# Input projection of a two-layer trunk: low-rank rows transposed before their norm, and three wide column sections in place of five

## The chip, the cores and the metric

The kernel runs on one core of one Trainium2 chip. The metric is the device time of one execution in microseconds (us), lower is better. Three runs of the kernel before gave 2254.48 to 2260.23 us, median 2259.06 us.

## The reference, cut to what matters

Two layers work on 512 latent and 256 context tokens of width 1024. Each layer projects the normed tokens to 2400 columns, cuts them into pieces, mixes the tokens in four ways (multi-head latent attention, neighbourhood attention, a bidirectional S5 recurrence, retention), and follows with a mixture of experts. The change touches the projection and the attention's two low-rank pieces, 192 columns of queries (cq) and 128 of keys and values (ckv):

```python
pl = split_cols(hl @ w_in[layer])
...
def mla_queries(cq, g_cq, w_uq, cos, sin):
    q = (rmsnorm(cq, g_cq) @ w_uq).reshape(B, L, MLA_HEADS, MLA_NOPE + MLA_ROPE)
...
def mla_keys_values(ckv, kr, g_ckv, w_ukv, cos, sin):
    kv = (rmsnorm(ckv, g_ckv) @ w_ukv).reshape(B, L, MLA_HEADS, MLA_NOPE + MLA_V)
...
def softmax_attention(q, k, v):
    s = jnp.einsum('bqhd,bkhd->bhqk', q, k, preferred_element_type=F32)
    p = jax.nn.softmax(s, axis=-1).astype(v.dtype)
```

`rmsnorm` multiplies each token's row by one number, the inverse root of its mean square. That number can also be applied after the matrix product.

## The kernel before, in words

One layer is `mixer`, then `moe`. In `mixer` the normed tokens lie transposed in SBUF, split into a high and a low part (`hTh`, `hTl`). A product with `w_in` is three matmuls (`mm3`, L202 to L204): high by high, high by low, low by high. The weights arrive raw by DMA on SP's queue (`wload`, L493) in pieces of half a section, into three buffers (`w_raw`). `wnext` splits each piece: ACT casts the high part (`w_hi`, L196), POOL subtracts it from the raw weights (`w_lo`, L197). `w_hi` and `w_lo` have four buffers each, two sections.

The projection goes in this order. First 256 columns for S5, transposed (`s5_in`); its result goes through DRAM into the tile `U`. Then the 1376 columns that are wanted with tokens on the partitions (`proj_nat`), in five sections of 288 or 272 columns (`SECS`); within a section each of the six token tiles takes 24 matmuls (8 chunks of the contraction by 3). In layer 1 the two context tiles skip columns that nobody needs. Last come three sections of 256 transposed columns (`proj_last`: keys, gate and queries).

S5 is woven in between. `s5_states` makes the states: matmuls `s_v` (L778) with matrices `Fg` that are read from DRAM by SP's queue (L775, two buffers), three copies of ACT into `H` for each, and then one long chain of small DVE operations on `H`: L790 to L793 seven steps within blocks of eight, L798 to L801 eleven steps over blocks, L806 to L809 the correction. ACT shifts the result into `HP` (L815 to L817). `s5_out` multiplies `HP` (matmuls `s_y`, L836 to L838, with `TPg` and `Eg` from SP's queue), applies the gelu, sends the result through DRAM into `GT`, and multiplies again (`s_z`, L858). `S5AT` says after which section each of the two is recorded; a list scheduler then sets every engine's order. In the kernel before they are recorded after section 0 and after section 2.

The two low-rank pieces go through `mla_prep` in every token tile: ACT squares the PSUM result and sums it (L1037), DVE adds epsilon (`rs_a`, L224), POOL raises it to the power of minus a half (`rs_b`, L226), DVE multiplies (`acn`, L1039), PE transposes it (`a_t`, L1042 and L1044), ACT applies the gains (`cqT`, `ckT`). The transposes are recorded a tile later (`flush`). In `mla_qkv` and `mla_attn`, some 140 us later, these feed the keys, values and queries and the softmax (`softmax`, L1002 to L1007).

Of the kernel before, what the change touches and what calls it, by code (L numbers as in the profile page):

```python
# [9 lines left out]
F32 = mybir.dt.float32  # L10
F32R = mybir.dt.float32r
# [4 lines left out]
ALU = mybir.AluOpType  # L16
# [18 lines left out]
SECS = (0, 288, 560, 832, 1104, 1376)  # L35
# [95 lines left out]
N_RQ, N_KR, N_CQ, N_NV, N_CKV, N_NW, N_RK, N_RV = 0, 256, 288, 480, 560, 688, 864, 1120  # L131
# [3 lines left out]
_ORDER = ("rq", "kr", "cq", "nv", "ckv", "nw", "rk", "rv", "u", "nq", "nk", "rg")  # L135
# [29 lines left out]
class Trunk:  # L165

    NB = ((7, 4, 3), (7, 6, 0))
    S5AT = ((0, 2), (0, 2))
# [156 lines left out]
    def mixer(self, l):  # L325
        tc, nc = self.tc, self.nc
        nt = self.nt
        with ExitStack() as left, ExitStack() as right:
            mS = self.pool("mS", es=left)
            self.mxS = mS.tile([P, 2, 2, nt * P], F32R, name="mixS")  # L330
            with ExitStack() as proj:
# [44 lines left out]
                with ExitStack() as sx:  # L376
                    na = self.pool("na", 2, es=sx, side="right")
                    self.s5u = self.pool("s5u", es=sx, side="right")
                    w = self.wnext()
                    self.s5_in(w, natP, self.s5u)  # L380
                    self.mla_prep_load(na)
                    for s in range(5):
                        self.proj_nat(s, na, tabs)
                        if s == self.S5AT[l][0]:
                            for _ in tabs:
                                pass
                            tb.close()
                            s5p, s5w = self.pool("s5p", es=sx, side="right"), self.pool("s5w", 2, es=sx, side="right")
                            self.s5_states(s5p, s5w)
                        if s == self.S5AT[l][1]:  # L390
                            self.s5_out(s5p, s5w)
# [124 lines left out]
    def proj_nat(self, s, na, side):  # L516
# [481 lines left out]
    def softmax(self, n, src, wk, tag):  # L998
# [6 lines left out]
        nc.scalar.activation(out=p, in_=src, func=AF.Exp, bias=nm, accum_out=s)  # L1005
# [61 lines left out]
    def mla_qkv(self, ap, aw):  # L1067
# [11 lines left out]
        self.aV = ap.tile([P, NT, 4, 64], F32, name="aV")  # L1079
        for i in range(NT):  # L1080
# [4 lines left out]
            nc.vector.tensor_copy(kf[:, :, 0:64], pv[:, :, 0:64])  # L1085
            nc.scalar.copy(out=self.aV[:, i], in_=pv[:, :, 64:128])
# [14 lines left out]
    def mla_attn(self, i, ap, aw):  # L1101
# [5 lines left out]
        for hp in range(2):  # L1107
            pTs = []
            for h in (2 * hp, 2 * hp + 1):
# [4 lines left out]
                p = self.softmax(T - k0, ps[:, :T - k0], aw, "a")  # L1114
# [765 lines left out]
def _layout(i):  # L1880
# [48 lines left out]
```

## Time and profile before

| what | value |
|---|---|
| median of three runs | 2259.06 us |
| the profiled execution's own time | 2260.11 us |
| its span, first to last instruction | 2258.3 us |
| busy: PE, DVE, ACT, POOL | 1955.8, 933.0, 499.6, 370.0 us |
| mean granted TensorE clock | 0.938 of full speed |
| projection and S5, layer 0 | about 92 to 299 us |
| projection and S5, layer 1 | about 1295 to 1488 us |
| attention of layer 0 | around 440 to 520 us |

The share of busy time is an average over stages with different limits; most of the span belongs to the experts, which the change does not touch. A row of a timeline gives the start, the duration, and in brackets how long the engine sat idle before and what ended that. A row of the windows gives each engine's busy time within a stretch (PE, its weight loads, DVE, ACT, POOL) and the clock that TensorE was granted in it: 1.00 is 2.4 GHz, 0.50 is 1.2 GHz. "issue" is an idle time for which the profile shows no releaser.

### The profile page before, as it was taken

The numbers are of one execution on the slowest core, as the hardware profiler recorded it, in microseconds if no ns is written. First come the engines' busy times: TensorE is split into PE (matmuls) and PEld (weight loads), VectorE is DVE, ScalarE is ACT, GpSimd is POOL, SyncE is SP. The second block draws the span as 40 slices with busy tenths as digits, with TensorE's granted clock in tenths as the row PEclk, the third lists the DMA queues.
The fourth block names the chain that finished last, engine by engine and source line by source line (L and its number), as shares of the span: only waits on it lengthen the run. The fifth ranks groups of instructions, "written<-read, shape, count | busy, mean of one in ns | idle before, by whom it ended". The sixth has DMA issues, their size and how long they took to land. (4 is left out here: it accounts for less than half of the span.)

```text
span 2258.3 us, 32874 instructions
## 1 busy us (share of the span) xinstructions
PE 1955.8 (87%) x12609; PEld 1161.1 (51%) x12609; DVE 933.0 (41%) x2175; ACT 499.6 (22%) x1095; POOL 370.0 (16%) x396
## 2 busy tenths in 40 slices
PE   5897988899869879989887887988896898998996
PEld 2787865457733323333332687855475454444443
DVE  3758156463425411111111529056544353453444
ACT  3342232251202200000001521332432111111111
POOL 2532252120100000000001322253302000000000
PEclk9898999999979999999998988989997899999998
DMA  7351355562568999999998441355617599999996
GB/s 271 107 150 44 83 175 195 194 202 71 191 248 305 376 391 375 385 375 362 373 373 342 154 105 49 83 166 192 202 59 269 216 395 419 419 420 418 419 420 255
DMA packets 160477, 578.55 MB, mean 256 GB/s; under 512 B 30032, under 2 KB 71504, under 8 KB 111152
## 3 DMA queue, kind: packets, MB, share of 16 engines
q1 hardware_dynamic: 123344, 530.69, 61.8%
q10 hardware_dynamic: 31296, 31.36, 4.5%
q0 software_dynamic: 5664, 14.23, 2.2%
q8 instruction: 104, 1.70, 0.3%
q14 instruction: 69, 0.57, 0.1%
HBM read 536.33 MB, written 43.42 MB: 257 GB/s over the span
## 5 line engine op out<-in xcount | busy, mean ns | idle before, releaser
L1671 PE MATMUL e_pa<-ew,hT 128*64 128x512 f32 x1664 | 424.4, 605 | 39.0 <-DMA ew<-in_moe_w 32.5
L1671 PEld LDWEIGHTS e_pa<-ew,hT 128*64 128x64 f32 x1664 | 126.2, 139 | 299.0 <-issue 245.1
L1695 PE MATMUL e_py<-ew,aT 128*64 128x512 f32 x832 | 207.1, 632 | 10.6 <-DVE aT L1687 7.8
L226 POOL TENSOR_TENSOR rs_b<-rs_a,mhalf 128x1 f32<-128x1 f32 (+1 forms) x58 | 38.2, 658 | 834.5 <-DVE rs_a L224 829.5
L202 PE MATMUL nat_ps<-w_hi,hTh 128*128 128x272 f32 (+3 forms) x480 | 149.4, 311 | 9.0 <-ACT nat L190 5.5
L1676 ACT ACTIVATE sA<-e_pa 64x512 f32<-64x512 f32 x52 | 30.8, 592 | 564.0 <-PE e_pa L1671 549.9
L1677 DVE TENSOR_TENSOR sA<-sA,e_pa 64x512 f32<-64x512 f32 x52 | 35.9, 690 | 277.2 <-ACT sA L1676 276.7
L204 PE MATMUL nat_ps<-w_hi,hTl 128*128 128x272 f32 (+3 forms) x480 | 147.1, 306 | 0.0
L203 PE MATMUL nat_ps<-w_lo,hTh 128*128 128x272 f32 (+3 forms) x480 | 146.8, 306 | 0.0
L197 POOL TENSOR_TENSOR w_lo<-w_raw,w_hi 128x1024 fp32r<-128x1024 f32 (+2 forms) x36 | 89.9, 2509 | 234.2 <-ACT w_hi L196 109.7
L1695 PEld LDWEIGHTS e_py<-ew,aT 128*64 128x64 f32 x832 | 59.0, 143 | 113.9 <-issue 95.2
L1557 POOL DMA_INDIRECT hg<-hd,stok x32 | 31.3, 980 | 446.2 <-PE hg_t L1569 411.9
L202 PEld LDWEIGHTS nat_ps<-w_hi,hTh 128*128 128x128 f32 x480 | 98.9, 206 | 10.7 <-ACT nat L190 6.4
L296 PE MATMUL mod_ps<-wmod,cT 128*32 128x256 f32 x768 | 80.1, 444 | 27.2 <-DMA wmod<-in_w_mod 27.2
L192 DVE COPY hT<-hg_t 128x256 f32<-128x256 f32 (+2 forms) x45 | 24.0, 534 | 192.0 <-PE e_pa L1671 160.6
L203 PEld LDWEIGHTS nat_ps<-w_lo,hTh 128*128 128x128 f32 x480 | 98.7, 206 | 0.4 <-issue 0.4
L204 PEld LDWEIGHTS nat_ps<-w_hi,hTl 128*128 128x128 f32 x480 | 98.4, 205 | 0.2 <-issue 0.2
L203 PE MATMUL tr_ps<-hTl,w_hi 128*128 128x256 f32 (+1 forms) x256 | 88.1, 344 | 11.0 <-POOL hTl L486 10.6
L202 PE MATMUL tr_ps<-hTh,w_hi 128*128 128x256 f32 (+1 forms) x256 | 88.1, 344 | 5.4 <-DVE gT L583 3.3
L204 PE MATMUL tr_ps<-hTh,w_lo 128*128 128x256 f32 (+1 forms) x256 | 85.5, 334 | 0.0
L1017 PE MATMUL pT_ps<-const,sm_p 128*128 128x128 f32 x352 | 57.6, 292 | 18.4 <-DVE sm_p L1007 12.1
L1642 DVE TENSOR_TENSOR xr<-xr,po_ps 128x512 f32<-128x512 f32 x104 | 67.1, 684 | 7.7 <-PE po_ps L1640 7.1
(471 smaller groups left out, 3530.6 us busy)
## 6 DMA issues: line engine op xcount, KB each, us to landing
ew<-in_moe_w SPq DMA_DIRECT2D x384, 1024.0 KB
wmod<-in_w_mod SPq DMA_DIRECT2D x96, 512.0 KB
yd<-zero SPq DMA_DIRECT2D x20, 512.0 KB
w_raw<-in_w_in SPq DMA_DIRECT2D x16, 544.0 KB
w_raw<-in_w_in SPq DMA_DIRECT2D x16, 512.0 KB
w_raw<-in_w_out SPq DMA_DIRECT2D x32, 256.0 KB
yd<-yA ACTq DMA_DIRECT2D x64, 128.0 KB
hd<-h ACTq DMA_DIRECT2D x10, 512.0 KB
```

The costliest lines, as they stand in the source:

```text
L197: (eng or self.nc.vector).tensor_tensor(out=lo, in0=src, in1=_f(hi), op=ALU.subtract)
L202: mm(out, lhsT=lh, rhs=rh, start=start, stop=False)
L203: mm(out, lhsT=lh, rhs=rl, start=False, stop=False)
L204: mm(out, lhsT=ll, rhs=rh, start=False, stop=stop)
L226: nc.gpsimd.tensor_tensor(out=r, in0=t, in1=self.mhalf[:, :n], op=ALU.pow)
L296: nc.tensor.matmul(ps[32 * j:32 * j + 32, 256 * q:256 * q + 256], lhsT=self.cT[:, k], rhs=w[:, j], start=(k == 0), stop=(k == KD - 1))
L1017: nc.tensor.transpose(pt[:, b], p[:, (a + b) * P:(a + b + 1) * P], self.ident)
L1557: self.nc.gpsimd.indirect_dma_start(out=hg, out_offset=None, in_=self.hd[0:n], in_offset=bass.IndirectOffsetOnAxis(ap=idx, axis=0), bounds ...
L1642: nc.vector.tensor_tensor(out=x, in0=x, in1=ps, op=ALU.add)
L1671: mm(pa[64 * j:64 * j + 64], lhsT=hT[k][:, 0:64], rhs=(w1, w3)[j][k], start=(k == 0), stop=(k == KD - 1))
L1677: nc.vector.tensor_tensor(out=sA, in0=sA, in1=pa[64:128], op=ALU.mult)
L1695: mm(py[64 * j:64 * j + 64, 0:512], lhsT=aT[:, k * 64:(k + 1) * 64], rhs=w2[k][:, h * 512:(h + 1) * 512], start=(k == 0), stop=(k == 3))
```

## The change

It does four things. (1) `mla_prep` copies the low-rank rows out of PSUM unnormed and transposes these; the sums of squares go into one tile of 12 columns for the layer (`cms`), and one `rsqrt` on it in `mla_qkv` gives all factors. The key and value factor is multiplied in where `kf` and `aV` leave PSUM; the query factor joins in the softmax, as a scale of the exponential and one more multiplication of the negated maximum for each of the 40 heads and tiles. (2) `proj_nat` has three sections of 464, 464 and 448 columns. The column order changes, so that a tile's results leave PSUM in eight pieces and not nine. (3) The weights come in quarters: each piece has half as many chunks, three raw buffers, five `w_hi` and six `w_lo` (four make a section). (4) The S5 parts are recorded after tile 3 of section 0 and after tile 4 of section 1.

```diff
-SECS = (0, 288, 560, 832, 1104, 1376)
+SECS = (0, 464, 928, 1376)
...
-    S5AT = ((0, 2), (0, 2))
+
+    S5AT = ((0, 3), (1, 4))
...
-        r = self.W.tile([P, 4, w], F32, tag="raw", name="w_raw", bufs=3)
...
+        r = self.W.tile([P, 2, w], F32, tag="raw", name="w_raw", bufs=3)
...
-        for a in range(2):
-            hi = self.W.tile([P, 4, w], F32R, tag="whi", name="w_hi", bufs=4)
-            lo = self.W.tile([P, 4, w], F32R, tag="wlo", name="w_lo", bufs=4)
+        for a in range(4):
+            hi = self.W.tile([P, 2, w], F32R, tag="whi", name="w_hi", bufs=5)
+            lo = self.W.tile([P, 2, w], F32R, tag="wlo", name="w_lo", bufs=6)
...
+            then(s, i)
...
+        if scale is not None:
+            nc.vector.tensor_tensor(out=nm, in0=nm, in1=scale, op=ALU.mult)
...
-        nc.scalar.activation(out=t[:, :w], in_=ps[:, :w], func=AF.Square, scale=w ** -0.5, accum_out=ss)
-        r = self.rsqrt(aw, ss, 1, 1.0, "ar")
-        nc.vector.tensor_scalar(out=t[:, :w], in0=ps[:, :w], scalar1=r, scalar2=None, op0=ALU.mult)
+        nc.scalar.copy(out=t[:, :w], in_=ps[:, :w])
         yield
+        sq = aw.tile([P, 192], BF16, tag="asq", name="asq", bufs=1)
+        nc.scalar.activation(out=sq[:, :w], in_=t[:, :w], func=AF.Square, scale=w ** -0.5, accum_out=self.cms[:, i + (0 if q else NT):i + (1 if q else NT + 1)])
...
+        rn = self.rsqrt(self.cp, self.cms, 2 * NT, 1.0, "ar")
+        self.rq, rk = rn[:, :NT], rn[:, NT:]
...
-            nc.vector.tensor_copy(kf[:, :, 0:64], pv[:, :, 0:64])
-            nc.scalar.copy(out=self.aV[:, i], in_=pv[:, :, 64:128])
+            nc.vector.tensor_scalar(out=kf[:, :, 0:64], in0=pv[:, :, 0:64], scalar1=rk[:, i:i + 1], scalar2=None, op0=ALU.mult)
+            nc.scalar.mul(out=self.aV[:, i], in_=pv[:, :, 64:128], mul=rk[:, i:i + 1])
...
-                p = self.softmax(T - k0, ps[:, :T - k0], aw, "a")
+                p = self.softmax(T - k0, ps[:, :T - k0], aw, "a", self.rq[:, i:i + 1])
```

Three places of the order that the scheduler sets. The first is SP's queue in layer 0 around the loads of `Fg` (each row a DMA; the numbers are those of buffers). Before:

```order
L493 DMA w_raw_764<-in_w_in 128x1088
L493 DMA w_raw_1518<-in_w_in 128x1088
L493 DMA w_raw_1524<-in_w_in 128x1088
L493 DMA w_raw_1771<-in_w_in 128x1088
L493 DMA w_raw_1777<-in_w_in 128x1088
L493 DMA w_raw_2179<-in_w_in 128x1088
L775 DMA Fg_1234<-s5f0_308 128x4x128
L775 DMA Fg_1244<-s5f0_308 128x4x128
L832 DMA TPg_2020<-s5k0_307 16x4x128 x3
L775 DMA Fg_1254<-s5f0_308 128x4x128
L775 DMA Fg_1264<-s5f0_308 128x4x128
```

With the change:

```order
L496 DMA w_raw_794<-in_w_in 128x928
L779 DMA Fg_1220<-s5f0_312 128x4x128
L779 DMA Fg_1230<-s5f0_312 128x4x128
L496 DMA w_raw_1566<-in_w_in 128x896
L496 DMA w_raw_1572<-in_w_in 128x896
L779 DMA Fg_1240<-s5f0_312 128x4x128
L779 DMA Fg_1250<-s5f0_312 128x4x128
L496 DMA w_raw_1578<-in_w_in 128x896
L496 DMA w_raw_1584<-in_w_in 128x896
L779 DMA Fg_1260<-s5f0_312 128x4x128
L779 DMA Fg_1270<-s5f0_312 128x4x128
L779 DMA Fg_1280<-s5f0_312 128x4x128
```

Before, all raw weights ahead stand in front of the `Fg` loads and none between them; with the change quarters of section 2 stand between the pairs of `Fg`.

The second is PE in layer 0 around the first matmuls on `HP` (L837 before, L841 with the change). Before:

```order
L203 MATMUL nat_ps_2480<-w_lo_2365,hTh_93 128x272
L837 MATMUL s5_y_2029<-HP_1503,Eg_2016 128x96
L204 MATMUL nat_ps_2480<-w_hi_2364,hTl_94 128x272
...
L204 MATMUL nat_ps_2480<-w_hi_2370,hTl_94 128x272
L202 MATMUL nat_ps_2506<-w_hi_2364,hTh_93 128x272
...
L838 MATMUL s5_y_2029<-HP_1503,Eg_2017 128x96
...
L204 MATMUL nat_ps_2506<-w_hi_2364,hTl_94 128x272
```

With the change:

```order
L205 MATMUL nat_ps_2170<-w_hi_2016,hTl_94 128x448
L841 MATMUL s5_y_1813<-HP_1489,Eg_1800 128x96
L203 MATMUL nat_ps_2170<-w_hi_2022,hTh_93 128x448
...
L205 MATMUL nat_ps_2170<-w_hi_2022,hTl_94 128x448
L203 MATMUL tr_ps_2230<-hTh_93,w_hi_2206 128x512
...
L842 MATMUL s5_y_1813<-HP_1489,Eg_1801 128x96
...
L203 MATMUL tr_ps_2230<-hTh_93,w_hi_2212 128x512
```

Before, 16 and 24 `nat_ps` matmuls of 272 columns come behind it (the rest of a tile and a whole tile); with the change 6 of 448 columns do, and then the section of the keys (`tr_ps`).

The third is PE in layer 0 between the last `s_y` (L838, now L842) and the first `s_z` (L858, now L862). Before:

```order
L838 MATMUL s5_y_2110<-HP_1503,Eg_2098 128x96
L203 MATMUL tr_ps_2606<-hTl_94,w_hi_2548 128x512
...
L202 MATMUL tr_ps_2632<-hTh_93,w_hi_2542 128x256
...
L202 MATMUL tr_ps_2670<-hTh_93,w_hi_2658 128x512
...
L202 MATMUL tr_ps_2698<-hTh_93,w_hi_2658 128x256
...
L202 MATMUL tr_ps_2726<-hTh_93,w_hi_2658 128x512
...
L204 MATMUL tr_ps_2726<-hTh_93,w_lo_2665 128x512
L858 MATMUL s5_z_2143<-GT_2134,wglu_2137 128x384 x2
```

With the change:

```order
L842 MATMUL s5_y_1894<-HP_1489,Eg_1882 128x96
L203 MATMUL tr_ps_2358<-hTh_93,w_hi_2334 128x512
...
L203 MATMUL tr_ps_2386<-hTh_93,w_hi_2334 128x256
...
L203 MATMUL tr_ps_2414<-hTh_93,w_hi_2334 128x512
...
L205 MATMUL tr_ps_2414<-hTh_93,w_lo_2353 128x512
L862 MATMUL s5_z_1927<-GT_1918,wglu_1921 128x384 x2
```

Before, the last group of `s_y` stands in the keys' third tile (`tr_ps_2606`), and 5 matmuls of 512 columns, 24 of 256, 24 of 512, 24 of 256 and 21 of 512 follow before `s_z`; with the change it stands three matmuls into the first tile of the gate (`tr_ps_2358`), and 21 of 512, 24 of 256 and 24 of 512 follow.

## Rows read from the trace of the kernel before

**Rows 1.** Windows by stage: window, length, engine busy us (instructions), TensorE clock, DMA share, GB/s

```profile
155.20:218.90 63.70, 52.10 (x371) 50.41 (x370) 59.49 (x173) 11.79 (x33) 12.91 (x9) 0.92 0.24 74
222.10:299.05 76.95, 72.82 (x437) 64.05 (x437) 8.60 (x12) 21.02 (x34) 17.50 (x15) 0.98 0.32 84
1295.26:1345.80 50.54, 43.75 (x294) 42.99 (x293) 5.87 (x30) 13.63 (x39) 15.00 (x17) 0.83 0.46 115
1345.80:1411.30 65.50, 52.10 (x367) 50.90 (x366) 60.48 (x175) 12.39 (x40) 14.17 (x11) 0.87 0.17 50
1414.60:1488.00 73.40, 71.76 (x435) 62.89 (x435) 8.26 (x11) 21.75 (x32) 19.69 (x13) 1.00 0.33 84
```

**Rows 2.** Waits of PE, 92 to 240 us: waiter, releaser, total us, times, longest

```profile
PE a_t L1042 <- DVE acn L1039: 6.1, 4, 2.5
PE s_y L837 <- issue: 1.8, 1, 1.8
```

**Rows 3.** The same, 1295 to 1440 us

```profile
PE a_t L1042 <- DVE acn L1039: 11.0, 3, 7.1
PE s_y L837 <- issue: 1.6, 1, 1.6
```

**Rows 4.** Timeline of PE: start us, us, operation; the first HP matmuls of layer 0

```profile
220.03 0.29 PE L203 MATMUL nat_ps<-w_lo,hTh 128*128 128x272 f32 x1
222.14 0.43 PE L837 MATMUL s_y<-HP,Eg 128*128 128x96 f32 x2 [1.82 <-issue]
```

**Rows 5.** Timeline of PE: 96 matmuls of 288 columns, 24 of 512

```profile
1295.26 0.30 PE L202 MATMUL nat_ps<-w_hi,hTh 128*128 128x288 f32 x1
...
1308.06 0.18 PE L202 MATMUL nat_ps<-w_hi,hTh 128*128 128x32 f32 x1
...
1450.39 0.40 PE L202 MATMUL tr_ps<-hTh,w_hi 128*128 128x512 f32 x1
...
1455.85 0.28 PE L202 MATMUL tr_ps<-hTh,w_hi 128*128 128x256 f32 x1
```

**Rows 6.** Groups of DVE by shape inside the chain of layer 0, 155.2 to 218.9 us

```profile
L1039 DVE TENSOR_SCALAR acn<-nat_ps,rs_b 128x128 f32<-128x128 f32 x5 | 1.7, 350 | 1.2 <-POOL rs_b L226 1.2
L224 DVE TENSOR_SCALAR rs_a<-ass 128x1 f32<-128x1 f32 x5 | 0.8, 153 | 0.0
```

**Rows 7.** Timeline of DVE: the same operation alone and beside a split

```profile
172.08 0.58 DVE L793 TENSOR_TENSOR H<-H,rt 128x192 f32<-128x192 f32 x1
...
174.77 2.58 DVE L793 TENSOR_TENSOR H<-H,rt 128x192 f32<-128x192 f32 x1
```

**Rows 8.** Timeline of POOL: the splits inside that chain

```profile
174.45 2.49 POOL L197 TENSOR_TENSOR w_lo<-w_raw,w_hi 128x1088 fp32r<-128x1088 f32 x1
203.61 4.69 POOL L197 TENSOR_TENSOR w_lo<-w_raw,w_hi 128x1024 fp32r<-128x1024 f32 x2 [20.26 <-ACT w_hi L196]
```

**Rows 9.** Timeline of PE: last L838 of layer 0, then its first L858

```profile
251.47 0.39 PE L838 MATMUL s_y<-HP,Eg 128*128 128x96 f32 x2
...
269.33 0.88 PE L858 MATMUL s_z<-GT,wglu 128*128 128x384 f32 x2 [0.29 <-DVE GT L846]
```

**Rows 10.** Timeline of PE in layer 1: the wait for Fg

```profile
1332.18 1.57 PE L778 MATMUL s_v<-U,Fg 128*128 128x96 f32 x6 [4.07 <-DMA Fg<-s5f]
```

**Rows 11.** Timeline of SP's queue ahead of that wait

```profile
1327.38 0.35 SPq L493 DMA_DIRECT2D w_raw<-in_w_in  x1
1327.83 1.16 SPq L775 DMA_DIRECT2D Fg<-s5f  x2
```

**Rows 12.** Windows: after that wait, and the attention stage

```profile
1332.20:1340.80 8.60, 8.60 (x48) 8.60 (x49) 0.00 (x0) 3.28 (x11) 0.00 (x0) 0.61 0.36 118
...
440.00:520.00 80.00, 77.25 (x446) 45.85 (x445) 47.30 (x98) 41.26 (x97) 21.20 (x19) 0.97 0.49 162
```

**Rows 13.** Waits of the SP queue, 40 to 310 us

```profile
SPq L493 <- POOL w_lo L197: 111.5, 12, 22.2
```

**Rows 14.** Groups of DVE by shape, 440 to 520 us

```profile
L1006 DVE RECIPROCAL sm_s<-sm_s 128x1 f32<-128x1 f32 x20 | 3.2, 159 | 4.9 <-ACT sm_p L1005 4.8
```

More of the change, by code (lines that the diff above doesn't have):

```diff
@@ L381, in mixer, with then @@
                     self.mla_prep_load(na)
-                    for s in range(5):
-                        self.proj_nat(s, na, tabs)
-                        if s == self.S5AT[l][0]:
+                    def then(s, i):
+                        if (s, i) == self.S5AT[0]:
                             for _ in tabs:
@@ L387, in mixer @@
                             tb.close()
[L388 to L391, printed above, removed]
+                            self.s5p, self.s5w = self.pool("s5p", es=sx, side="right"), self.pool("s5w", 2, es=sx, side="right")
+                            self.s5_states(self.s5p, self.s5w)
+                        if (s, i) == self.S5AT[1]:
+                            self.s5_out(self.s5p, self.s5w)
+                    for s in range(len(SECS) - 1):
+                        self.proj_nat(s, na, tabs, then)
                 nat2 = self.pool("nat2", es=rt, side="right")
@@ L489, in wload @@
     def wload(self, c0, w, a):
-        r = self.W.tile([P, 4, w], F32, tag="raw", name="w_raw", bufs=3)
-        o = c0 * D + a * 512 * w
-        self.nc.sync.dma_start(out=r.rearrange("p k n -> p (k n)"), in_=self.I["w_in"][self.l, o:o + 512 * w].rearrange("(p n) -> p n", p=P))
+        r = self.W.tile([P, 2, w], F32, tag="raw", name="w_raw", bufs=3)
+        o = c0 * D + a * 256 * w
+        self.nc.sync.dma_start(out=r.rearrange("p k n -> p (k n)"), in_=self.I["w_in"][self.l, o:o + 256 * w].rearrange("(p n) -> p n", p=P))
         return r
@@ L497, in wstart @@
         self.secs = [(T_U, 256)] + [(a, b - a) for a, b in zip(SECS[:-1], SECS[1:])] + [(T_NK, 256), (T_RG, 256), (T_NQ, 256)]
-        self.ahead = [self.wload(*self.secs[0], a) for a in range(2)]
+        self.ahead = [self.wload(*self.secs[0], a) for a in range(4)]
     def wnext(self):
@@ L509, in wnext @@
                 ahead.append(self.wload(*self.secs[0], a))
-            for k in range(4):
+            for k in range(2):
                 his.append(hi[:, k])
@@ L514, in wnext, with proj_nat @@
         return his, los
-    def proj_nat(self, s, na, side):
+    def proj_nat(self, s, na, side, then):
         nc = self.nc
@@ L530, in proj_nat @@
             self.flush()
-            next(side, None)
-            next(side, None)
+            for _ in range(3):
+                next(side, None)
             for p0, w, dst in ((N_RQ, 256, self.nat[:, i, 0]), (N_KR, 32, None), (N_CQ, 192, None), (N_NV, 80, 0), (N_CKV, 128, None),
@@ L995, in retention, with softmax @@
             yield
-    def softmax(self, n, src, wk, tag):
+    def softmax(self, n, src, wk, tag, scale=None):
         nc = self.nc
@@ L1024, in mla_prep_load @@
         self.krt = [self.load_const(na, n) for n in ("krc", "krs")]
+        self.cms = self.cp.tile([P, 2 * NT], F32, tag="cms", name="cms%d" % l)
+        nc.gpsimd.memset(self.cms, 1.0)
         self.gq = na.tile([P, 3], F32, name="gcq", bufs=1)
@@ L1032, in mla_prep @@
         nc, gq = self.nc, self.gq
-        w = 192 if which == N_CQ else 128
+        q = which == N_CQ
+        w = 192 if q else 128
         tk = slice(i * P, (i + 1) * P)
-        ss = aw.tile([P, 1], F32, tag="ass", name="ass")
         t = aw.tile([P, 192], F32, tag="acn", name="acn")
-        nc.scalar.activation(out=t[:, :w], in_=ps[:, :w], func=AF.Square, scale=w ** -0.5, accum_out=ss)
-        r = self.rsqrt(aw, ss, 1, 1.0, "ar")
-        nc.vector.tensor_scalar(out=t[:, :w], in0=ps[:, :w], scalar1=r, scalar2=None, op0=ALU.mult)
+        nc.scalar.copy(out=t[:, :w], in_=ps[:, :w])
         yield
+        sq = aw.tile([P, 192], BF16, tag="asq", name="asq", bufs=1)
+        nc.scalar.activation(out=sq[:, :w], in_=t[:, :w], func=AF.Square, scale=w ** -0.5, accum_out=self.cms[:, i + (0 if q else NT):i + (1 if q else NT + 1)])
         pt = self.pT.tile([P, 512], F32, tag="T", name="a_t")
```

10 lines of the change are left out of this document (5 added, 5 removed).

## The prediction

> **What bounds the kernel now.** I read the windows by stage first, then the waits of PE in the two projection stages, then the timelines of DVE, POOL and PE at the places where a wait ends. The experts, most of the span, are untouched, so the question is two stages of about 200 us each.
>
> I cut each at the chain's start and at `s_y`; the windows of layer 1 show all three parts, those of layer 0 the last two [rows 1]. In the middle part DVE is busy 59.49 of 63.70 us in layer 0 and 60.48 of 65.50 us in layer 1: that is S5's chain, from its first multiplication at 155.2 (1345.8) to its last addition at 218.9 (1411.3). PE is busy 52 us in it and loses time in small waits: 6.1 us for `acn` in layer 0, 11.0 in layer 1 [rows 2, 3]. These look like the cost that the change takes away. But PE also waits at the end of the chain, 1.8 and 1.6 us at the first `s_y` on `HP` [rows 2, 3]; in layer 0 the matmul before it starts at 220.03, and it starts at 222.14, 3.2 us after the chain's end at 218.9 [rows 4]. (The profile calls that releaser "issue"; the ACT copies into `HP` lie in these 3.2 us.) So PE's small waits and the chain end together: **the chain sets the time, and PE's slack is already used up**. The reader should see that taking work or waits from PE ahead of `s_y` moves them into the wait at `s_y`. What counts is when the chain starts, how long it is, and what PE must still do behind it.
>
> **The change, part by part.** Matmuls: five sections become three, so the two layers' 1440 matmuls become 864 for the same columns. 96 matmuls of 288 columns take 12.80 us, 0.1333 each, and 24 of 512 take 5.46, 0.2275 each [rows 5]; between them 464 columns come to 0.208, 448 to 0.201, 272 to 0.127. Layer 0: 144 x 0.1333 + 576 x 0.127 = 92.4 against 288 x 0.208 + 144 x 0.201 = 88.8 us, 3.6 saved; in layer 1, with its shorter context tiles, it is about 10. Nearly all of it is ahead of `s_y`, and so are all `acn` waits: I count neither as a gain but where it moves the chain's start.
>
> Layer 0, start of the chain. PE reaches the first `s_v` after 144 matmuls of 0.208 and 26 more, 35.4 us, where it took 144 x 0.1333 + 113 x 0.127 = 33.5: +1.9. The first split of S5's own weights handles half as much: POOL takes 2.49 us for 1088 elements [rows 8], so 1.2 for 512 where it took 2.3 for 1024: up to -1.2, and the `acn` waits ahead of `s_v` give a little. I take +0.3; the bounds are -4 (PE alone sets the pace of the `s_v`) and +6 (below, the SP queue).
>
> Layer 0, the chain. Five sets of `rs_a` and `acn` go: 0.8 + 1.7 busy and 1.2 waiting [rows 6], -3.7. Splits on POOL stretch the chain: `H<-H,rt` takes 2.58 us beside a 2.49 us split and 0.58 alone [rows 7, 8], so 2.0 of 2.49, 0.80 of POOL's time. Now 2.49 twice (one of them stands there) and 4.69 for a pair [rows 8], 9.67 us of splits, lie in the chain; with the change three quarters of section 2 and one of the keys, 3 x 2.05 + 1.2 = 7.4 (by 2.49/1088 per element): -1.8. Chain -5.5.
>
> The Trainium skill ("SBUF — State Buffer", section "Who interferes with whom") says that a VectorE instruction with two SBUF inputs and a GpSimd one that reads SBUF exclude each other for the whole instruction. By that rule the whole of POOL's time would count, not 0.80 of it, and the sum below would be 0.8 us higher, as layer 1 gains more splits than layer 0 loses; the trace bears the rule out in kind, but the row shows 2.0 of 2.49.
>
> Layer 0, behind `s_y`. 40 matmuls of 272 columns followed, 5.1 us, now 6 of 448, 1.2: -3.9. The way from the last `s_y` to `s_z` takes 17.7 us, `s_z` waits 0.29 of them [rows 9]; it is the gelu and two trips through DRAM. Matmuls of 17.1 us covered it, now 21 x 0.2275 + 24 x 0.120 + 24 x 0.2275 = 13.1: +4.3, a new wait. After PE has waited 4.07 us for `Fg` in layer 1 [rows 10], the next 8.6 us run at a clock of 0.61 [rows 12], at a loss of 3.4 us (0.50 is 1.2 GHz, 1.00 is 2.4). A wait of some 17 us at `s_y` will do the same; layer 0 now runs at 0.98 behind `s_y` [rows 1], 1.5 us lost, so +1.9. Two more splits that nothing covers at the step from keys to gate, a quarter each: +1.5 (0 to 4). Sum of layer 0: 0.3 - 5.5 - 3.9 + 4.3 + 1.9 + 1.5 = -1.4.
>
> Layer 1, start. Now the chain starts 50.5 us after the stage's first matmul, at a mean clock of 0.83 [rows 1]; 4.07 of it are the wait for `Fg`, which stood behind a raw weight on SP's queue until 1327.83 [rows 10, 11], and 3.4 the slow clock after it [rows 12]. With the change four tiles of section 0, 96 x 0.208 = 20.0 us, then four pairs of `s_v` which in layer 0 are now 15.8 us from first to last. The U tile's loads and the raw quarters between the `Fg` will keep some of the waits; from 36 (these alone) and 50.5 I take 41.7: **-8.8** (-13 to 0).
>
> Layer 1, the chain. Seven `acn` sets of about 0.75 us by rows 6, -5.2, and a little more for idle steps, -6.0; but eight quarters of 2.0 to 2.1 us lie in it, as PE now runs through three sections: 15.8 us against some 9.9, x 0.80: +4.7. Chain -1.3. Behind `s_y`: 134 matmuls of 272 columns, 17.0 us, now 110 of 448, 22.1: +5.1. Slow clock after a wait of over 20 us, where it is 1.00 now [rows 1]: +3.4. Splits: +1.5. Sum: -8.8 - 1.3 + 5.1 + 3.4 + 1.5 = -0.1.
>
> Attention: 40 multiplications of 128x1 on DVE. A reciprocal of that shape takes 0.159 us [rows 14]: 6.4 us if all lie on the path, 0 if none. PE is busy 77.25 of 80 us in that stage and DVE 47.30 [rows 12], so I take 0; DVE has room. If PE lost that cover, the 6.4 would be the price. The factors on `kf` and `aV` replace copies of the same shape, and the one `rsqrt` replaces 22: 0.
>
> Sum: -1.4 - 0.1 = -1.5. The profiled execution took 2260.1, so 2258.6; it lies 1.05 above the median of the runs, so **2257.5 us**. About 0.3%, 6.8 us, is what a measurement of this kernel can tell from no change: from 2252.3 to 2265.9 it is the same.
>
> **The rivals.** *Faster*: what I put down as new waits does not come. The raw quarters never hold `Fg`, so layer 0's chain starts 4 us earlier and layer 1's 4 more, and the splits at the section steps are covered (3 us): 2257.5 - 11 = 2246. For it: SP's waits for raw buffers, 111.5 us in 12 [rows 13], end sooner with pieces half as long. Against it: `w_hi` and `w_lo` now hold one section and a quarter, where they held two.
>
> *Slower*, one mechanism: on SP's queue in layer 0 quarters of section 2 stand between the pairs of `Fg`. The fourth needs the raw buffer of the first, whose split needs a `w_hi` that PE frees only with section 0, and ACT, which then copies `H`. The longest such wait is 22.2 us now [rows 13], with nothing urgent behind. If the first split of section 2 ends after about 143 us, when the third pair of `Fg` is due, each microsecond more is one of the chain: 6 in layer 0, 4 in layer 1, and 3.4 for the clock after the wait at `s_v`: 2257.5 + 13.4 = 2271. From 8.4 us together it reads as slower.
>
> *Attention*: the 6.4 us of DVE all on the path, 2264, the same.
>
> *The change does what it says in the order, but PE's waits only change their name*: that is the forecast.
>
> **How the numbers follow.** Forecast 0.42 (its own range 2251 to 2264), faster rival 0.28, slower rival 0.22, attention 0.08. The forecast gives 0.05 to faster and 0.02 to slower. Faster: 0.28 + 0.05, rounded to 0.34; slower 0.22 + 0.02 = 0.24; the same 0.42. The range reaches from 3 below the faster rival to 1 above the slower: 2243 to 2272.
>
> **What would show it.** No `a_t` waits for DVE; a wait of over 10 us of PE at the first `s_y` in both layers, then a clock near 0.6; matmuls of 464 columns 0.208 apart; chains of about 58 and 64 us that start near 155.5 and 1337; a wait of some 4 us at `s_z` in layer 0. I am wrong if PE is not idle at `s_y`, if the `s_v` wait for `Fg` over 5 us in layer 0, or if the chain in layer 1 is shorter than 60 us.

## The result, and the profile after

The changed kernel took 2272.96 us (median of 9 runs, 2265.71 to 2277.93), against 2260.23 us of 9 runs of the kernel before beside it: a ratio of 1.0062, 95% interval 1.0046 to 1.0078. It is slower by 0.6%, some 14 us. The forecast was no change, 2257.5 us in a range up to 2272; the slower rival's 2271 was the nearest number, but not for its reason.

The profiled execution has a span of 2271.5 us, 13.2 more than before. The table cuts both traces at the first start of a PE tile; each entry is the length of a stretch in us. Stretches without projection, retention and attention do the same work in both, but for a few splits of weights, and differ by -6.3 and +3.1; so a difference of a few us in one stretch of two profiles can be scatter (e1 below has more on this). The differences add up to 12.5; the first `tr_ps` starts 0.7 later.

| stretch | before | after | difference |
|---|---|---|---|
| layer 0: first `tr_ps` to first `nat_ps` | 48.4 | 42.4 | -6.0 |
| layer 0: first `nat_ps` to first `n_s` (projection, S5) | 206.6 | 208.4 | +1.8 |
| layer 0: first `n_s` to first `a_kv` (neighbourhood attention, retention) | 140.6 | 143.1 | +2.5 |
| layer 0: first `a_kv` to first `wo_ps` (attention) | 89.0 | 89.3 | +0.3 |
| from there to the first `tr_ps` of layer 1 | 743.3 | 737.0 | -6.3 |
| layer 1: `tr_ps` to `nat_ps` | 23.3 | 23.7 | +0.4 |
| layer 1: `nat_ps` to `n_s` | 192.7 | 199.0 | +6.2 |
| layer 1: `n_s` to `a_kv` | 108.4 | 113.2 | +4.8 |
| layer 1: `a_kv` to `wo_ps` | 73.4 | 79.0 | +5.6 |
| from there to the end | 588.6 | 591.7 | +3.1 |

The projection of layer 1 as a window, before (`nat_ps` to `n_s`; columns as in [rows 1]):

```profile
1295.30:1488.00 192.70, 169.29 (x1105) 158.26 (x1103) 75.00 (x216) 50.91 (x113) 49.31 (x45) 0.91 0.30 79
```

And after: the whole, the part from the last `s_v` to the first `s_y` on `HP`, and the part from there to `n_s`:

```profile
1288.70:1487.70 199.00, 162.53 (x817) 139.71 (x815) 75.48 (x198) 54.84 (x128) 54.32 (x47) 0.91 0.33 89
1332.30:1401.70 69.40, 46.47 (x230) 40.15 (x228) 62.71 (x162) 21.77 (x65) 21.11 (x15) 0.85 0.18 54
1401.70:1487.70 86.00, 80.84 (x411) 68.70 (x411) 9.06 (x14) 23.12 (x37) 22.36 (x20) 0.96 0.36 96
```

PE is busy 6.8 us less than before, and idle 36.5 us (199.0 - 162.5) where it was idle 23.4. The saving on matmuls came, and twice as much idle time with it. The last window answers to layer 1's last one of [rows 1]: 86.0 us where it was 73.4, at a clock of 0.96 where it was 1.00.

What PE waits for in layer 1 after the change, 1290 to 1520 us (answers to [rows 3]):

```profile
PE nat_ps L203 <- DVE nat L193: 13.6, 3, 9.3
PE r_kv L945 <- DVE d L927: 5.6, 1, 5.6
PE s_z L862 <- DVE GT L850: 4.5, 1, 4.5
PE nat_ps L204 <- POOL w_lo L198: 3.6, 4, 1.8
PE s_v L782 <- DMA Fg<-s5f: 3.5, 4, 1.8
...
PE s_y L841 <- POOL rs_b L227: 3.2, 1, 3.2
```

The waits for `acn` on DVE are gone. In their place PE waits 13.6 us for evacuations of `nat_ps`. The longest ends at 1389.73 on the timeline of PE:

```profile
1389.73 0.74 PE L203 MATMUL nat_ps<-w_hi,hTh 128*128 128x448 f32 x1 [9.32 <-DVE nat L193]
```

and DVE's timeline says what it waited for:

```profile
1379.28 2.17 DVE L802 TENSOR_TENSOR bt<-H,s5pw 128x16 f32<-128x16 f32 x2
1381.38 3.31 DVE L810 TENSOR_TENSOR fx<-H,s5pw 128x1232 f32<-128x1232 f32 x1
1384.61 2.04 DVE L804 TENSOR_TENSOR bt<-bt 128x16 f32<-128x16 f32 x1
...
1388.02 1.44 DVE L811 TENSOR_TENSOR fx<-H,s5pw 128x1232 f32<-128x1232 f32 x1
1389.37 0.17 DVE L804 TENSOR_TENSOR bt<-bt 128x16 f32<-128x16 f32 x1
1389.45 0.22 DVE L193 COPY nat<-nat_ps 128x64 f32<-128x64 f32 x1
...
1394.13 1.43 DVE L810 TENSOR_TENSOR fx<-H,s5pw 128x1232 f32<-128x1232 f32 x1
```

A copy of 64 columns, 0.22 us, stands in DVE's order between S5's operations, and PE, without a free PSUM buffer, waits 9.32 us for its turn. It is this long in part because POOL splits four quarters of weights at that moment:

```profile
1379.15 8.69 POOL L198 TENSOR_TENSOR w_lo<-w_raw,w_hi 128x896 fp32r<-128x896 f32 x4 [22.62 <-ACT w_hi L197]
```

Beside these splits L810 takes 3.31 us, and alone, at 1394.13, 1.43. With the two of L802, L804 and L805 (2.17, 2.04 and 1.20 us; 0.29, 0.17 and 0.18 alone) some 6.6 us are added ahead of the copy, an estimate from these times.

Behind this wait PE reaches the first `s_y` on `HP` and waits 3.20 us once more. The profile names `rs_b` there, but ACT's copy into `HP` ends in the same moment, at 1401.59:

```profile
1400.54 1.05 ACT L821 COPY HP<-H 64x1024 f32<-64x1024 f32 x1
```

In layer 0 the wait at the first `s_y` is short, 2.48 us, and `a_t` waits 5.3 us for ACT's copy into `acn`, where it waited 6.1 for DVE. A wait at `s_z` has come in both layers (from PE's timeline; answers to [rows 4, 9]):

```profile
214.67 0.43 PE L841 MATMUL s_y<-HP,Eg 128*128 128x96 f32 x2 [2.48 <-ACT HP L821]
...
262.64 1.19 PE L862 MATMUL s_z<-GT,wglu 128*128 128x384 f32 x2 [3.13 <-DVE GT L850]
...
1450.48 1.13 PE L862 MATMUL s_z<-GT,wglu 128*128 128x384 f32 x2 [4.47 <-DVE GT L850]
```

Behind the projection, from `n_s` to `a_kv`, PE is not idle for longer: 22.0 us before and 21.4 after in layer 0, 19.9 and 20.1 in layer 1. Its busy time has grown, by 3.1 and 4.6 us, at a lower granted clock. Windows, layer 0 before and after, layer 1 before and after, and layer 1 of e5 (below):

```profile
299.05:439.60 140.55, 118.55 (x960) 72.08 (x961) 88.40 (x266) 45.06 (x120) 51.53 (x74) 0.94 0.62 204
295.55:438.60 143.05, 121.66 (x960) 74.80 (x960) 87.57 (x266) 44.99 (x120) 51.04 (x74) 0.92 0.61 194
1488.00:1596.40 108.40, 88.50 (x701) 56.12 (x701) 71.35 (x195) 34.30 (x88) 46.57 (x69) 0.88 0.58 186
1487.70:1600.90 113.20, 93.06 (x701) 58.86 (x701) 68.70 (x191) 34.15 (x88) 42.50 (x67) 0.84 0.54 164
1483.20:1595.50 112.30, 91.03 (x701) 57.08 (x701) 71.44 (x196) 34.64 (x88) 46.63 (x69) 0.85 0.56 180
```

In layer 0 the order of PE, DVE, ACT and POOL in this stretch is the same in both kernels. In layer 1 it differs, but e5, which has the order of the kernel before there, is 3.9 us longer too, at 0.85. So it is not shown that the change costs these 7 us.

The one clear gain is at the start of layer 0. PE's waits there, before (44.1 to 92.5 us) and, in the second fence, after (44.8 to 87.2):

```profile
PE tr_ps L203 <- POOL hTl L486: 10.6, 8, 4.2
```

```profile
PE tr_ps L204 <- DVE hTl L489: 4.2, 3, 3.1
PE tr_ps L204 <- POOL hTl L489: 3.0, 7, 0.8
```

Between PE's first and last `tr_ps` of this product POOL did three splits of weights before, 7.9 us, and does two after, 3.5 us (one more starts at the very end of each): with one section and a quarter of `w_hi` it can't run as far ahead, and POOL is free for the split of the hidden rows (`hTl`) that PE waits for. The gain is some 4 to 6 us: e2, e5 and e7, which have the order of the kernel before in this stretch, take 46.2 to 46.3 us and not 48.4. Groups of POOL by shape, before, then after:

```profile
L486 POOL TENSOR_TENSOR hTl<-hf,hTh 128x256 fp32r<-128x256 f32 x18 | 21.4, 1200 | 8.8 <-DVE hTh L192 4.6 <-ACT hTh L190 2.9 <-DVE t L671 0.7
L197 POOL TENSOR_TENSOR w_lo<-w_raw,w_hi 128x1152 fp32r<-128x1152 f32 x2 | 5.4, 2722 | 1.0 <-ACT w_hi L196 1.0
```

```profile
L489 POOL TENSOR_TENSOR hTl<-hf,hTh 128x256 fp32r<-128x256 f32 x18 | 17.8, 1006 | 13.1 <-DVE hTh L193 9.0 <-ACT hTh L191 2.8 <-ACT F L733 1.3
L198 POOL TENSOR_TENSOR w_lo<-w_raw,w_hi 128x928 fp32r<-128x928 f32 x2 | 4.4, 2190 | 8.0 <-ACT w_hi L197 8.0
```

In the attention of layer 1 (1600.9 to 1679.8) the 16 heads have a new operation on DVE and a longer exponential on ACT:

```profile
L1008 DVE TENSOR_TENSOR sm_nm<-sm_nm,rs_b 128x1 f32<-128x1 f32 x16 | 4.2, 263 | 0.2
```

```profile
L1011 ACT ACTIVATE sm_p<-a_s,sm_nm,rs_b 128x768 f32<-128x768 f32 x16 | 15.9, 992 | 7.6 <-DVE sm_nm L1008 7.5
```

Before, the exponential took 902 ns, and ACT waited 3.6 us for its maxima:

```profile
L1005 ACT ACTIVATE sm_p<-a_s,sm_nm 128x768 f32<-128x768 f32 x16 | 14.4, 902 | 3.6 <-DVE sm_nm L1002 3.6
```

### The profile page after: what moved, and what is told of

Its sections match the earlier page's. It is cut to its first block, busy times and chain, and to the rows that moved or that the text cites. A ratio compares the mean times of both kernels' runs of the same rounds, so it can differ in the third digit from the quotient of the medians.

```text
span 2271.5 us, 31746 instructions
## 1 busy us (share of the span) xinstructions
PE 1955.3 (86%) x12033; PEld 1133.6 (50%) x12033; DVE 926.0 (41%) x2167; ACT 511.3 (23%) x1131; POOL 361.4 (16%) x398
## 5 line engine op out<-in xcount | busy, mean ns | idle before, releaser
L1706 PE MATMUL e_py<-ew,aT 128*64 128x512 f32 x832 | 206.4, 631 | 9.6 <-DVE aT L1698 8.4
L227 POOL TENSOR_TENSOR rs_b<-rs_a,mhalf 128x1 f32<-128x1 f32 (+2 forms) x38 | 30.3, 798 | 759.6 <-DVE rs_a L225 752.8
L198 POOL TENSOR_TENSOR w_lo<-w_raw,w_hi 128x512 fp32r<-128x512 f32 (+2 forms) x56 | 94.9, 1714 | 239.6 <-ACT w_hi L197 117.0
L203 PE MATMUL nat_ps<-w_hi,hTh 128*128 128x464 f32 (+3 forms) x288 | 111.7, 388 | 17.7 <-DVE nat L193 13.6
L204 PE MATMUL nat_ps<-w_lo,hTh 128*128 128x464 f32 (+3 forms) x288 | 111.2, 386 | 7.5 <-POOL w_lo L198 7.5
L1706 PEld LDWEIGHTS e_py<-ew,aT 128*64 128x64 f32 x832 | 58.4, 143 | 113.2 <-issue 96.8
L205 PE MATMUL nat_ps<-w_hi,hTl 128*128 128x464 f32 (+3 forms) x288 | 109.2, 379 | 0.0
L203 PEld LDWEIGHTS nat_ps<-w_hi,hTh 128*128 128x128 f32 x288 | 58.3, 202 | 25.1 <-DVE nat L193 14.6
L1023 PEld LDWEIGHTS pT_ps<-const,sm_p 128*128 128x128 f32 x352 | 43.4, 153 | 50.9 <-issue 30.4
L1651 PE MATMUL po_ps<-Yh,ohT 128*128 128x512 f32 (+1 forms) x128 | 53.9, 430 | 15.8 <-DVE xr L1653 9.3
```

The lines of the kernel that those rows point to most:

```text
L198: (eng or self.nc.vector).tensor_tensor(out=lo, in0=src, in1=_f(hi), op=ALU.subtract)
L203: mm(out, lhsT=lh, rhs=rh, start=start, stop=False)
L204: mm(out, lhsT=lh, rhs=rl, start=False, stop=False)
L205: mm(out, lhsT=ll, rhs=rh, start=False, stop=stop)
L1023: nc.tensor.transpose(pt[:, b], p[:, (a + b) * P:(a + b + 1) * P], self.ident)
L1651: nc.tensor.matmul(ps[:, q * o - 512 * c:q * o - 512 * c + o], lhsT=ohT[:, (i * m + q) % 8], rhs=y[:, q * o:q * o + o], start=(z == 0), st ...
```

## The experiments

The medians below stand beside the kernel before on the same chip; the ratio is to that kernel, with its 95% interval. The changed kernel's is 1.0062.

Theory A: the factor in the softmax costs. Theory B: the three sections and the new places of S5 cost. The first four kernels were to part the two.

**e1, the factor left out.**

```diff
-                p = self.softmax(T - k0, ps[:, :T - k0], aw, "a", self.rq[:, i:i + 1])
+                p = self.softmax(T - k0, ps[:, :T - k0], aw, "a")
```

> The changed kernel with the query factor left out of the softmax (the output then lacks the norm of the queries): 40 multiplications of 128x1 and the scale of the exponential are gone, nothing else. Theory A (the factor lies on each head's chain of maximum, multiplication, exponential, and costs 5.6 us in layer 1's attention): the stretch from the first a_kv to the first wo_ps of layer 1 goes back from 79 to 73 or 74 us, and the time from 2273 to about 2267. Theory B (the loss is in the projection and S5): 2272 to 2274, the stretch stays at 78 to 79.

Measured: 2260.44 us, ratio 1.0015 (0.9995 to 1.0034), lower than A said. The attention of layer 1 is back at 73.5 us, that of layer 0 goes from 89.3 to 87.7: 7.1 of the 12.5 us. ACT waits for its maxima as before, and its exponential is as short:

```profile
L1011 ACT ACTIVATE sm_p<-a_s,sm_nm 128x768 f32<-128x768 f32 x16 | 14.4, 902 | 3.6 <-DVE sm_nm L1006 3.5
```

The rest lies in no stretch that e1 touches, and one profile can't place it: the profiled execution of e1 has a span of 2265.0 us, above its median, and 212.2 us in layer 0's projection, where the order of all four engines is that of the changed kernel, which took 208.4. So a stretch of one profile is known to some 4 us, no better.

**e2, the new norm alone**: the kernel before with the new `mla_prep`, `mla_qkv` and `softmax`.

```diff
+        nc.scalar.copy(out=t[:, :w], in_=ps[:, :w])
...
+            nc.vector.tensor_tensor(out=nm, in0=nm, in1=scale, op=ALU.mult)
```

> The kernel before with the new mla_prep, mla_qkv and softmax alone: five sections, halves, old places of S5. Theory A: the waits for acn go, but the chain still ends at the same place, less some 4 us for the acn sets; attention of layer 1 costs 5.6 more: 2258 to 2264. Theory B: the norm part is harmless or a gain, at or below 2257.

Measured: 2261.28 us, ratio 1.0016 (0.9995 to 1.0037), where A said. Layer 1's projection goes from 192.7 to 189.3 us, its attention from 73.4 to 75.7, which is 2.3 more and not 5.6.

**e3, sections, quarters and places of S5 alone**: the changed kernel with the old norm.

```diff
-SECS = (0, 288, 560, 832, 1104, 1376)
+SECS = (0, 464, 928, 1376)
...
-    S5AT = ((0, 2), (0, 2))
+    S5AT = ((0, 3), (1, 4))
```

> The changed kernel with the old mla_prep, mla_qkv and softmax: three sections, quarters, new places of S5. Theory A: without the factor in the softmax 2266 to 2268, even though the acn waits come back. Theory B: the whole loss or more, 2273 to 2280.

Measured: 2277.68 us, ratio 1.0086 (1.0053 to 1.0118). This is B: this half of the change loses alone at least about as much as the whole (the intervals overlap). In layer 1's projection PE is busy 160.1 us and idle 41.3; its waits there, with 23.4 us for `acn` where the kernel before has 11.0:

```profile
1294.70:1496.10 201.40, 160.10 (x817) 137.62 (x815) 78.58 (x217) 52.56 (x118) 61.01 (x56) 0.90 0.32 88
```

```profile
PE a_t L1046 <- DVE acn L1043: 23.4, 3, 12.6
```

**e4, late query rows**: the changed kernel, but the query rows stay unnormed in SBUF until `mla_qkv`, where they are multiplied by their factor and transposed. The softmax is the old one.

```diff
+        for i in range(self.nt):
+            self.mla_cq(i, aw)
...
+        nc.vector.tensor_scalar(out=t, in0=self.cqN[:, i], scalar1=self.rq[:, i:i + 1], scalar2=None, op0=ALU.mult)
+        pt = self.pT.tile([P, 4, P], F32, tag="T", name="a_t")
+        nc.tensor.transpose(pt[:, 0], t[:, 0:P], self.ident)
```

> The changed kernel, but the query rows are kept unnormed, and are multiplied by their factor and transposed in mla_qkv (12 transposes, 6 multiplications per layer), so the softmax is the old one. Theory A: attention of layer 1 from 79 to 74 or 75 us, 2267 to 2269. Theory B: 2272 to 2275.

Measured: 2257.73 us, ratio 1.0000 (0.9983 to 1.0018), more than A said. Attention of layer 1 takes 72.6 us; the late rows' transposes stand ahead of its `a_kv`, in the stretch before, which takes 112.0. The projection of layer 1 takes 187.2, where the query transposes were in it 199.0, with 27.3 us of idle PE instead of 36.5.

**e5, the factor alone**, a constant one, in the kernel before.

```diff
+        if scale is not None:
+            nc.vector.tensor_tensor(out=nm, in0=nm, in1=scale, op=ALU.mult)
...
+                p = self.softmax(T - k0, ps[:, :T - k0], aw, "a", self.one1)
```

> The kernel before, with the new softmax alone, its factor a constant one: the 40 multiplications and the scale operand of the exponential, nothing else. Theory A (each head's chain becomes longer by the multiplication, 0.25 to 0.29 us, and 0.09 us of exponential): 16 heads of layer 1 cost 5.5 us, the 24 of layer 0 less than 2, so 2264 to 2267. Theory B (the factor is hidden, and its removal gained through another order of the scheduler): 2258 to 2261.

Measured: 2259.34 us, ratio 0.9993 (0.9976 to 1.0010): at most 2.3 us slower, as B said. Yet in its profile the attention of layer 1 takes 76.8 us and that of layer 0 89.8, 3.4 and 0.8 more than before. That the heads of layer 1 get longer is seen in three pairs (e1, e2, e5), by 5.4, 2.3 and 3.4 us; that this costs the kernel as much is not shown.

**e6, quarters alone**, in the kernel before, with six raw, eight high and eight low buffers (two sections, as before).

```diff
-            hi = self.W.tile([P, 4, w], F32R, tag="whi", name="w_hi", bufs=4)
+            hi = self.W.tile([P, 2, w], F32R, tag="whi", name="w_hi", bufs=8)
```

> The kernel before with weights in quarters alone (six raw, eight high and eight low buffers: the same memory, two sections ahead). Theory A (three wide sections with little weight ahead cost, quarters gain 5 to 6 us at the start of layer 0, where the stretch from the first tr_ps to the first nat_ps goes from 48 to 42 us): 2252 to 2255. Theory B (quarters themselves cost, by twice as many splits in the chain's way): 2262 or more.

Measured: 2262.16 us, ratio 1.0005 (0.9986 to 1.0025): the number is at B's edge, but it can't be told from the kernel before, so it supports neither theory. The start of layer 0 is as long as before, 48.5 us: not the quarters shorten it.

**e7, late query rows in five sections**: the kernel before with e4's norm.

> The kernel before with unnormed low-rank rows, the query rows normed and transposed in mla_qkv, no factor in the softmax; five sections, halves. Theory A: no acn waits, no factor, but the chain decides: 2254 to 2258. Theory B (the order of the scheduler decides): anywhere from 2250 to 2266.

Measured: 2247.05 us, ratio 0.9937 (0.9917 to 0.9958), better than A's range and **faster than both kernels**. It differs from e2 in the query rows alone: factor in the softmax there, late rows here, and 1.0016 became 0.9937, some 18 us. From the changed kernel to e4 the same step gave 14. PE is idle 19.7 us in layer 1's projection:

```profile
1283.80:1471.40 187.60, 167.87 (x1096) 156.31 (x1094) 72.66 (x197) 50.72 (x115) 46.12 (x36) 0.92 0.31 81
```

**e8, the same with the quarters of e6.**

> The same with weights in quarters (six raw, eight high and eight low). Theory A: both gains add up, 2247 to 2252. Theory B: 2258 or more.

Measured: 2252.51 us, ratio 0.9978 (0.9956 to 1.0000). Late rows seem to gain again (the interval ends at 1.0000); quarters with long lookahead add nothing to them, as e7 is lower.

The next theories were on the place of `s5_out`. Theory C: the scheduler puts `s_y` too early in PE's order; 110 matmuls that could fill the chain stand behind it. Theory D: PE has no free time in the chain, since evacuations hold it.

**e9, s5_out later, in the changed kernel.**

```diff
-    S5AT = ((0, 3), (1, 4))
+    S5AT = ((0, 3), (2, 5))
```

> The changed kernel with s5_out recorded after the last token tile of section 2 (S5AT second entry 2, 5): no nat_ps matmul is left behind the first s_y on HP in layer 1, where 110 were. Theory C (PE is idle in the chain because the scheduler put s_y too early): the nat_ps move into idle time, the stretch from nat_ps to n_s of layer 1 goes from 199 to about 185, the time to 2259. Theory D (PE is held in the chain by PSUM evacuations that queue behind the chain on DVE, 13.6 us in layer 1, so it has no free time for them): 197 to 200, the time 2270 to 2275.

Measured: 2258.26 us, ratio 0.9995 (0.9982 to 1.0008): the time that C gave, and the whole loss is gone. But C's mechanism is not what the trace shows: the projection of layer 1 takes 195.7 us, not 185, and the waits for evacuations stay, as D said:

```profile
PE nat_ps L203 <- DVE nat L193: 12.4, 3, 7.8
PE a_t L1051 <- ACT acn L1046: 4.7, 1, 4.7
```

`s_z` now waits 1.36 us and not 4.47, and the stretch behind the projection takes 108.1 us and not 113.2 in layer 1, 140.3 and not 143.1 in layer 0. There PE's granted clock is back at 0.88 and 0.94, and in layer 0 no engine's order has changed. So C's time came without C's reason: 3.3 us of the 15 lie in layer 1's projection, the rest in parts of up to 5 us, each near what one profile can tell.

**e10, and evacuations by ACT alone.**

```diff
-                    self.evac(dst[:, x0 - p0:x1 - p0], src)
+                    self.evac(dst[:, x0 - p0:x1 - p0], src, 2)
```

> The same, and proj_nat's results leave PSUM by ACT alone (before, ACT and DVE in turn). Theory D: the waits nat_ps on DVE nat go, all nat_ps end before the chain, the stretch of layer 1 goes from 199 to 183 to 187 and the time to 2257 to 2261. Theory C: the same as the run before it, within 4 us. Rival: ACT is then late with the w_hi casts and H copies, and the time does not fall.

Measured: 2256.24 us, ratio 0.9990 (0.9972 to 1.0008). Layer 1's projection takes 193.7 us, not D's 183 to 187: as C said, little changes. The wait only changes its engine. ACT's order has the six copies into `HP` ahead of two evacuations, and ACT stands still until the chain ends, so that PE waits 11.95 us for those:

```profile
PE nat_ps L203 <- ACT nat L191: 11.9, 1, 11.9
```

So here the wait does not hang on the engine that empties PSUM, but on the scheduler's order of it against the chain.

**e11 and e12, the same two changes on e7** (five sections, late rows; `S5AT` second entry at the end of the last section, e12 also with ACT alone).

> The kernel of e7 (five sections, halves, late query rows) with s5_out recorded after section 4: 38 and 134 matmuls behind s_y become none. Theory C: layer 1 gains up to 15 us, 2232 to 2238. Theory D: 2245 to 2249.

> The same with proj_nat's results leaving PSUM by ACT alone. Theory D: layer 1 gains some 15 us and layer 0 some 4 against e7: 2228 to 2235. Theory C: as the run before it.

Measured: 2260.05 us, ratio 1.0005 (0.9994 to 1.0015), and 2260.19 us, 1.0004 (0.9988 to 1.0020). Both theories miss: on e7 the later place loses some 15 us, where on the changed kernel it won 15. Layer 1's projection takes 193.5 us where e7 took 187.6, layer 0's 210.0 against 206.4; the profiled execution of e11 is its fastest (2250.85), so the stretches show only part of the loss.

**e13, e4 and e9 together.**

> The changed kernel with late query rows (e4) and with s5_out recorded after section 2 (e9), each of which alone closed the gap to the kernel before. Additive causes (the factor with its transposes some 14 us, the place of s5_out 14 us): 2243 to 2248. One cause seen twice (both only undo the same collision behind the chain in layer 1): 2255 to 2260.

Measured: 2252.65 us, ratio 0.9972 (0.9958 to 0.9986), between the two. From 1.0062 the two changes take 0.0062 and 0.0067 alone and 0.0090 together, so they don't add: in part they undo the same loss. Idle time of PE in layer 1's projection is 32.1 us.

**e14, the short lookahead alone**: the kernel before with the changed kernel's buffers.

```diff
-            hi = self.W.tile([P, 4, w], F32R, tag="whi", name="w_hi", bufs=4)
-            lo = self.W.tile([P, 4, w], F32R, tag="wlo", name="w_lo", bufs=4)
+            hi = self.W.tile([P, 2, w], F32R, tag="whi", name="w_hi", bufs=5)
+            lo = self.W.tile([P, 2, w], F32R, tag="wlo", name="w_lo", bufs=6)
```

> The kernel before with the changed kernel's weight buffers alone: quarters, three raw, five high, six low, five sections of 288 or 272. If the short lookahead is what frees POOL at the start of layer 0: the stretch from the first tr_ps to the first nat_ps there 42 us, not 46 to 48. If it also costs splits inside the projection: the stretches from nat_ps to n_s longer than 206.6 and 192.7 by 4 to 9. Sum 2254 to 2264; above 2268 the buffers, not the three sections, carry e3's loss.

Measured: 2249.62 us, ratio 0.9954 (0.9935 to 0.9973), a gain where no theory had more than a few us. The start of layer 0 takes 41.4 us, as expected, the projection of layer 0 214.8, 8 more, that of layer 1 186.9, 6 less, and the stretch behind it 104.5, 4 less:

```profile
1297.20:1484.10 186.90, 168.37 (x1104) 156.23 (x1103) 76.62 (x221) 56.29 (x133) 59.12 (x67) 0.93 0.38 101
```

e3 differs from this kernel in the three sections (with their column order) and the place of S5, and is slower by 1.3% of the kernel before (1.0086 against 0.9954).

**e15, the same on e7.**

> The kernel of e7 with those buffers. If the gain at the start of layer 0 adds to e7: 2241 to 2246. If the splits cost more: 2250 or above.

Measured: 2254.73 us, ratio 0.9979 (0.9962 to 0.9995). The gains of e7 and e14 don't add: e7 alone is better than both together, and e14 seems so (the intervals overlap).

## Why the prediction was wrong

*What held.* The `acn` waits on DVE went and gave nothing, as put down; the matmul saving did not reach the end. Layer 0 behind `s_y` was forecast 3.8 us longer, as -3.9, +4.3, +1.9 and +1.5, and is 4.0 longer (76.9 to 80.9 us from `s_y` to `n_s`). The sum is nearer than its terms: the granted clock there went from 0.98 to 0.94 without the wait of 17 us that was to lower it. The `s_z` wait of layer 0 was put at 4.3 and is 3.13. The chain of layer 0, `s_v` end to `s_y`, got 4.1 us shorter, forecast 5.5; its start, forecast 0.3 later, came 1.9 later. The chains on DVE take 59.6 and 66.6 us, forecast about 58 and 64. Slow clock after the long waits of layer 1 came: 0.96 behind `s_y` where it was 1.00.

*The wait that was put in the wrong place.* That "the chain sets the time, and PE's slack is already used up" held for the time: `s_y` starts when ACT's copies into `HP` are done, in layer 1 at 1401.69 after a copy that ends at 1401.59. What failed is what was to follow from it, that PE's idle time appears as one wait at `s_y`, of some 17 us in layer 0 and over 20 in layer 1. By the prediction's own terms layer 0 had only some 9 us for it (a chain of 58.2 and 3.2 more, less 52.2 of matmuls). PE is idle 22.9 us from the last `s_v` to `s_y` in layer 1, but only 3.20 of them at `s_y`, and 2.48 in layer 0. The rest lies in the chain, where three PSUM buffers are full and the copy that frees one stands behind S5's operations and POOL's splits. The forecast counted what PE must do and when the chain ends. It did not ask which evacuations stand behind the chain on DVE. e10 shows that another engine's order does the same. What these waits cost is not shown: in this order a shorter one would have left a longer wait at `s_y`, and e9, which loses nothing against the kernel before, still has 12.4 us of them.

*The term on layer 1*, -0.1, is the first step that failed: it is +6.2 in the trace. Of its three parts, the start came 6.4 us earlier, not 8.8 (`nat_ps` to the last `s_v`, 49.2 to 42.8); the chain up to `s_y` got 0.2 longer, not 1.3 shorter, as its eight splits took 17.7 us and not 15.8; and behind `s_y` it is 12.5 longer, not 10.0, since a wait of 4.47 us at `s_z`, which was forecast for layer 0 alone, came in layer 1 too. Each is off by 1.5 to 2.5 us, all the same way.

*The step on attention*, "so I take 0; DVE has room", is the second: a busy share says nothing on a chain of single operations within one head. The upper bound, 6.4 us, was the right end to take for the trace of the changed kernel (+5.6 and +0.3). Its price was also short: the multiplication takes 263 ns on average in layer 1, not 159, and the exponential 90 ns more for its scale, which was counted at nothing. That the whole kernel pays it is shown only together with other parts of the change: without the factor the changed kernel gets some 11 us back (e1), and late rows in place of the factor gain 14 and 18 us (the changed kernel against e4, e2 against e7), of which the transposes that leave the projection are a part; alone the factor cost at most 2.3 us (e5).

*What the sum left out*: the stretch behind the projection, neighbourhood attention and retention. It is 2.5 and 4.8 us longer, at a lower granted clock (0.92 for 0.94, 0.84 for 0.88) and with no more idle time of PE. In layer 0 no engine's order changed there. In layer 1 it did, and PE waits 5.61 us at `r_kv` for `d`, but other waits are shorter by as much. Why the clock was lower stays open; with e9 it is back (140.3 and 108.1 us).

*The balance*, from one profile each: -1.5 forecast, then +5.9 for attention, +6.3 for layer 1's term, +3.2 for layer 0's (+1.8, not -1.4), +7.3 for the stretch behind and -6.0 for the start of layer 0; the other stretches, -2.8 together, are within what two profiles of the same work differ by. That gives the 12.5 of the table to 0.1.

*What came out better*: the start of layer 0, -6.0 where at most -1.2 was seen in it. The rows of `hTl` on POOL were not looked at; the splits of the next sections that the short lookahead forbids were what held them (e14 against e6).

*The rivals.* The slower one's number was near (2271), its mechanism not: the waits for `Fg` in layer 0 are 0.9 us in all. The attention rival, 2264 with a chance of 0.08, had its price about right, but not the rest. The sentence on the Trainium skill's page ("SBUF — State Buffer", section "Who interferes with whom") can stand: in the changed kernel three operations of layer 0's chain from 173.79 on, with POOL at its splits, take 2.23, 2.27 and 2.09 us, and 0.36 to 0.53 just before (in layer 1 the 6.6 us beside 8.69 of splits are 0.77 of POOL's time), but neither figure for it would have changed the sum by more than 0.8 us.

*What stays open*: which of the scheduler's many moves, and how much of the granted clock, make up the 14 us. Removing the factor (e1), delaying the query rows (e4) and moving `s5_out` (e9) each bring back 10 to 15 us, together less than their sum (e13), and the last loses some 15 on the five sections (e11). With the old norm the three sections with their place of S5 carry the loss (e3 against e14); which of the two does was not parted.

## What to carry to other kernels

When engines run in order, ask of each producer not only how much work it has left while a long chain runs elsewhere, but which small operations that free its buffers stand behind that chain: time saved on the matmuls can come back as idle time there, and POOL's splits beside the chain make it longer (9.32 us for a copy of 0.22). Moving such a wait gained nothing by itself here (e10). A scalar that moves out of one stage is priced in the chain where it arrives, by the latency of one head, not by the busy share of its engine. Here the better place was late and once per token tile: e7 is 0.63% under the kernel before, and with the factor in the softmax in its place (e2) nothing was gained.

## What was not expected

Less lookahead made a kernel faster: with buffers for one section and a quarter in place of two sections e14 gains 0.46%. In its profile the first product of layer 0 takes 41.4 us in place of 48.4 (with two sections of lookahead in quarters it is 48.5, e6), and the trace's reason is that POOL splits fewer weights ahead of the rows that PE waits for. But the projection of layer 0 gives back these 7 us and one more; the gain that remains is in layer 1, 5.8 and 3.9 us from `nat_ps` to `a_kv`, and its cause is open. On e7 the same buffers lose 0.4% (e15). And the place where a block of work is recorded moved the time by -15 us in one kernel (e9) and +15 in another (e11), with the same matmuls. Last, kernels with the same order of all four engines in a stretch differ there by 2 to 4 us from profile to profile (e1, e5).
